# A decoder layer on one core: where the loads between the retention heads stand, gated values in quarters, mixing's weights before the last head

## The chip, the core and the metric

The kernel runs on one core of one Trainium2 chip. The core has five engines with a queue each, and each takes its instructions in the order of its queue: TensorE (PE; its weight loads are shown as PEld) for matmuls, VectorE (DVE), ScalarE (ACT), GpSimd (POOL), and SyncE (SP), which here only issues DMA transfers. ScalarE and GpSimd can issue transfers too; such an issue stands in the engine's own queue and is shown as ACTq or POOLq. The metric is the device time of one execution in microseconds (us), as a median over runs. The trace comes from one more execution under the hardware profiler.

## The reference

One layer of a decoder for 512 prompt tokens and 8 sequences of 8 new tokens, 576 tokens in all, width 1024, float32. Between two gated feed-forward blocks of half weight stands the token mixing, which is the part that matters here:

```python
z = h @ w_in
u, v, q, k, rv, rg, ga, gb = jnp.split(z, SPLIT_POINTS, axis=-1)
u = jax.nn.gelu(u)
v = layer_norm(jax.nn.gelu(v), gm_ln_g, gm_ln_b)
o_a = u * chunk_spatial_mix(v, gm_ws, gm_bs)
qh = rotary(q.reshape(B, L, RET_HEADS, RET_DK), pos)
kh = rotary(k.reshape(B, L, RET_HEADS, RET_DK), pos) * (RET_DK ** -0.5)
o_r, S_new = retention(qh, kh, vh, S0)
o_b = head_rms(o_r).reshape(B, L, RET_V).astype(h.dtype) * jax.nn.silu(rg)
merged = jax.nn.sigmoid(ga) * (o_a @ w_a) + jax.nn.sigmoid(gb) * (o_b @ w_b)
```

Retention has 8 heads with keys of 128 and values of 256 columns and works in chunks of 128 tokens: scores with a decay inside a chunk, and a state of 128 x 256 from chunk to chunk. The new tokens start from a given state for each sequence and head (8 x 8 states of 128 x 256) and give back the new ones. The spatial mixing multiplies the normalised values v in 8 groups of 128 columns by a masked 128 x 128 matrix over the tokens of a chunk, adds a bias, and multiplies by u.

## The kernel before, in words

Products keep float32 accuracy by splitting each operand into a high part, rounded to the matmul's format (fp32r), and the rest. A product is three matmuls: high x high, high x rest, rest x high. A weight is loaded into a raw buffer (`load_raw`, L139, SP's queue; three buffers `wraw`), ScalarE writes its high part (L150) and VectorE its rest (L151) into one of four buffers `whl`. Results are split the same way by `split` (L158 on ScalarE, L159 on VectorE). `proj` (L447) is the product of a weight with 288 token columns at a time; two halves make 576.

The first part of the kernel, up to about 760 us, makes the adaptive gains, the first feed-forward block and the products for q, k, rg, ga and gb, which it writes to DRAM. The last part, from about 1238 us, is the product with w_a, the merge, w_o and the second feed-forward block. The change lies between, in the loop over the heads (L1599) and in the mixing behind it (L1627 to L1694). A turn of the loop for head `hd` does:

- the two weight pieces of the value projection (`load_w`, L1601), and the fetch of the next head's four row tensors q, k and two of rg (`fetch`, L1279, SP's queue);
- the rotary of this head's q and k (`rotary`, L1284 to L1286 on VectorE, L1287 on GpSimd), ahead of the value projection, except for head 0, where it stands behind it;
- the value projection itself (`values_of`, L1309 for four blocks of 128 tokens, L1320 for the new tokens);
- what is left of the head before (`finish(prev)`), and then this head's `core`, a generator in eight pieces. Its pieces are put between the products that run beside it: after each group of matmuls `tick` counts an assumed time down, and a generator whose pause has run out gives its next piece. The pieces: scores (L1337, L1339), decayed q and k, transposes; states of the chunks (L1399, L1404); product with the old states of the new tokens (L1415); outputs for each half of 128 columns (L1428 to L1443, copies L1432, L1448, squares L1449, gate L1488); sum of squares (L1451) and its split; its column sums (L1461), the new states (L1472, L1476) and their way out (L1477, GpSimd's queue), the reciprocal root (L1465); and the scaling of the outputs (L1481 to L1489) with their split into `OB`;
- beside it the products: for heads 0 and 1 the values v (`values`, L1532), for heads 2, 4 and 6 the product of two finished heads with w_b (`out_b`, four pieces), for heads 3 and 5 four pieces of u (`gate_u`); for head 7 nothing.

The states of the next head (`states`: one constant tile, L1292, and four tiles of 256 KB, L1296) are issued at the end of `core` in ScalarE's queue. Their four buffers are those that the old states leave by L1477. `values` loads four pieces of 512 columns x 2 blocks, which fill all four `whl`. `layer_norm` starts behind head 1's values, loads gain and bias for each half (L1569, L1570), normalises ten tiles (L1575, L1578) and writes them to DRAM.

Behind the loop the mixing loads the ten value tiles back (L1632), then a mask, the small and the large mixing weights and the bias (L1634 to L1641). `masks` (L1645, L1647) is called between the two pieces of `out_b` for head 6, and `mix` for eight groups (L1662, L1664 matmuls, L1666, L1670 bias, L1674 product with u on GpSimd, then `split`) runs while head 7's core ends; the two pieces of `out_b` for head 7 come behind groups 5 and 6.

Most row-sized tiles come from one pool of 36 slots (`slot`). The order on the engines' queues isn't simply the source's: a planner takes the traced instructions, gives each an assumed cost and, going through that assumed time, puts the earliest in the source that could start next on each engine; a tile is given to an instruction when one is free in that plan. On the chip each queue then keeps that order, whatever the real times are.

## Time and profile before

| what | us |
|---|---|
| runs: median (lowest, highest), 3 runs | 1743.71 (1738.88, 1744.86) |
| the profiled execution's own time | 1748.43 |
| its span, from the first to the last instruction | 1746.6 |
| TensorE busy in the span | 1670.1 |
| stretch of the heads and the mixing, 759.9 to 1238.0 | 478.1 |
| TensorE busy before it, of 759.9 | 740.7 |
| TensorE busy behind it, of 508.6 | 497.1 |
| mean granted TensorE clock | 0.978 |

How to read the rows: a row of the timeline has the start, the duration of the merged group, engine, line, operation, tiles written and read, shape and count; in brackets the time that the engine sat idle before it and what released it. Rows of stretches have the length, the busy time of the five engines in the order PE, PEld, DVE, ACT, POOL with their counts, the granted clock as a share of full speed, the busy share of the DMA engines and GB/s. Rows of waits have the total, the number and the longest. The durations of merged matmuls overlap by a little at their ends, so the distance between starts is the better measure of their pace.

### The profile page before, as it was taken

Reading aid. Unit: us, or ns where it says so; the run is one execution under the profiler, and the core shown is the slowest. Engines: PE = TensorE matmul, PEld = TensorE weight load, DVE = VectorE, ACT = ScalarE, POOL = GpSimd, SP = SyncE. Lnnn points to the kernel's source line nnn. Section 1 sums busy time; section 2 is a strip of 40 time slices with the busy share of each in tenths; the row PEclk is TensorE's granted clock in tenths of the full one; section 3 lists DMA queues with packets and bytes.
Section 4 is the critical chain, followed back from the end, with each engine's and each line's share of the span. In section 5 each row is a group of like instructions: output and inputs, shape, how many; then the busy total and the mean of one; then the engine's idle time right before and its main releaser. Section 6 shows DMA issues by size and latency. Waiting matters only on the chain.

```text
span 1746.6 us, 30913 instructions
## 1 busy us (share of the span) xinstructions
PE 1670.1 (96%) x12324; PEld 1590.7 (91%) x12324; DVE 1150.3 (66%) x1813; ACT 787.6 (45%) x1335; POOL 304.4 (17%) x384
## 2 busy tenths in 40 slices
PE   7999999999999999989989999977999999999997
PEld 4889999999999998978788899977999999999997
DVE  6857847675787776745577545555566968676773
ACT  5534515344655556533344444433335625334454
POOL 0000000001211010022334344444512000000002
PEclk9999999999999999999999999987999999999999
DMA  9443544434366676673266475695951232222331
GB/s 304 138 133 97 151 127 124 132 86 133 95 200 205 209 208 183 200 237 107 72 224 205 155 162 160 149 236 130 275 174 52 70 100 85 85 85 86 96 97 55
DMA packets 299314, 254.41 MB, mean 146 GB/s; under 512 B 13721, under 2 KB 256665, under 8 KB 299170
## 3 DMA queue, kind: packets, MB, share of 16 engines
q1 hardware_dynamic: 273922, 198.20, 37.9%
q0 software_dynamic: 14320, 43.33, 9.4%
q10 hardware_dynamic: 10928, 10.91, 2.0%
q8 instruction: 96, 1.57, 0.4%
q14 instruction: 48, 0.39, 0.1%
HBM read 207.01 MB, written 45.38 MB: 145 GB/s over the span
## 4 chain that ended last, share of the span: by engine, by line
PE 74%; issue 9%; DMA 7%; DVE 5%; POOL 3%; ACT 2%; SPq 0%; POOLq 0%; ACTq 0%; DVEq 0%
PE ps L613 35%; PE ps L447 28%; PE ps L1309 2%; PE ps L1532 2%; PE ps L269 2%; DMA ada<-in_w_ada_dram 1%; PE ps L1399 1%; DMA ut_ret_state_sample_dram<-S 1%; DMA c<-x1d 1%; DMA xa<-in_w_ada_dram 1%; DMA v<-vd 1%; POOL c L1287 1%; POOL c L1488 1%; DMA S<-in_state_ret_dram 1%; DMA c<-in_gm_ln_g_dram 1%
## 5 line engine op out<-in xcount | busy, mean ns | idle before, releaser
L613 PE MATMUL ps<-xa,whl 128*128 128x288 f32 x3000 | 428.2, 297 | 4.5 <-ACT whl L631 1.4
L613 PEld LDWEIGHTS ps<-xa,whl 128*128 128x128 f32 x3000 | 408.9, 189 | 17.1 <-issue 5.9
L613 PE MATMUL ps<-xs,whl 128*128 128x288 f32 x2040 | 294.9, 297 | 2.1 <-ACT sn L622 1.9
L613 PEld LDWEIGHTS ps<-xs,whl 128*128 128x128 f32 x2040 | 279.0, 189 | 15.0 <-ACT sn L622 7.0
L641 DVE TENSOR_TENSOR whl<-wraw,whl 128x1024 fp32r<-128x1024 f32 x192 | 234.7, 1225 | 54.0 <-ACT whl L631 48.6
L631 ACT CAST whl<-wraw 128x1024 fp32r<-128x1024 f32 x192 | 200.2, 1048 | 104.6 <-DVE wraw L755 61.7
L447 PE MATMUL ps<-c,wd 128*128 128x288 f32 x1824 | 245.7, 295 | 0.0
L447 PEld LDWEIGHTS ps<-c,wd 128*128 128x128 f32 x1824 | 242.8, 188 | 2.7 <-issue 1.7
L447 PE MATMUL ps<-c,whl 128*128 128x288 f32 x1368 | 195.9, 302 | 8.3 <-ACT c L158 8.0
L447 PEld LDWEIGHTS ps<-c,whl 128*128 128x128 f32 x1368 | 189.0, 194 | 10.3 <-ACT c L158 8.4
L434 POOL TENSOR_TENSOR x<-x,s 128x64 f32<-128x64 f32 x72 | 35.4, 492 | 822.1 <-DVE s L433 822.0
L428 DVE SCALAR_TENSOR_TENSOR x<-ps,gate,x 128x288 f32<-128x288 f32 (+1 forms) x128 | 61.1, 481 | 118.3 <-PE ps L447 118.3
L151 DVE TENSOR_TENSOR whl<-wraw,whl 128x1024 fp32r<-128x1024 f32 x56 | 78.5, 1402 | 73.0 <-ACT whl L150 72.5
L622 ACT COPY sn<-ps 128x288 f32<-128x288 f32 x195 | 77.4, 399 | 104.1 <-PE ps L613 103.2
L914 ACT CAST wd<-wraw 128x640 fp32r<-128x640 f32 (+2 forms) x58 | 45.3, 781 | 110.3 <-PE ps L447 106.2
L1309 PE MATMUL ps<-whl,xx 128*128 128x256 f32 x768 | 89.4, 277 | 0.0
L1309 PEld LDWEIGHTS ps<-whl,xx 128*128 128x128 f32 x768 | 88.8, 188 | 0.2
L150 ACT CAST whl<-wraw 128x1024 fp32r<-128x1024 f32 x56 | 58.3, 1049 | 49.1 <-PE ps L1320 16.1
L613 PE MATMUL ps<-xs,whs 128*128 128x288 f32 x480 | 70.4, 295 | 0.0
L631 ACT CAST whs<-wraw 128x512 fp32r<-128x512 f32 x62 | 38.4, 620 | 65.9 <-PE ps L613 59.0
L613 PEld LDWEIGHTS ps<-xs,whs 128*128 128x128 f32 x480 | 65.8, 188 | 0.8 <-issue 0.8
L919 DVE TENSOR_TENSOR wd<-wraw,wd 128x640 fp32r<-128x640 f32 (+2 forms) x58 | 54.0, 931 | 10.8 <-ACT wd L914 10.7
(282 smaller groups left out, 2246.0 us busy)
## 6 DMA issues: line engine op xcount, KB each, us to landing
ada<-in_w_ada_dram SPq DMA_DIRECT2D x56, 512.0 KB, 4.4
wraw<-in_w_in_dram SPq DMA_DIRECT2D x96, 256.0 KB, 4.1
wraw<-in_w_gate_dram SPq DMA_DIRECT2D x88, 256.0 KB, 3.0
wraw<-in_w_up_dram SPq DMA_DIRECT2D x88, 256.0 KB, 3.9
wraw<-in_w_in_dram SPq DMA_DIRECT2D x32, 512.0 KB, 5.1
wraw<-in_w_down_dram SPq DMA_DIRECT2D x32, 384.0 KB, 3.7
accd<-c POOLq DMA_DIRECT2D x40, 288.0 KB, 4.8
wraw<-in_w_down_dram SPq DMA_DIRECT2D x32, 320.0 KB, 3.3
```

Of the source, the lines that this page charges most:

```text
L150: ACT.copy(out=hi, in_=raw)
L151: (eng or DVE).tensor_tensor(out=lo, in0=raw, in1=hi.bitcast(F32), op=ALU.subtract)
L428: DVE.scalar_tensor_tensor(out=x[:, o:o + w], in0=ps[:, :w], scalar=g[:, c, 0:1], in1=x[:, o:o + w], op0=ALU.mult, op1=ALU.add)
L434: return lambda: POOL.tensor_tensor(out=x[:, NP:T], in0=x[:, NP:T], in1=u, op=ALU.add)
L447: PE.matmul(ps[:, :H], lhsT=s[:, k, c0:c0 + P], rhs=m[:, HALF[h]], start=k == 0 and z == 0, stop=k == kc - 1 and z == 2,)
L613: PE.matmul(ps[:, :H], lhsT=s[:, j * P:(j + 1) * P], rhs=m[:, j, :], start=fresh and j == 0 and z == 0, stop=j == 3 and z == 2, skip_group ...
L622: ACT.copy(out=t, in_=ps[:, :H])
L631: ACT.copy(out=hl[:, 0], in_=src)
L641: DVE.tensor_tensor(out=hl[:, 1], in0=src, in1=hl[:, 0].bitcast(F32), op=ALU.subtract)
L914: ACT.copy(out=hl[:, 0], in_=self.raw[c])
L919: DVE.tensor_tensor(out=lo, in0=self.raw[c], in1=hi.bitcast(F32), op=ALU.subtract)
L1309: PE.matmul(ps[:, :DV], lhsT=s, rhs=m, start=i == 0, stop=i == 23)
```

## The change

States are issued on SP's queue for every head, behind the two weight loads of the value projection. The fetch of the next head's rows stands behind the first of the products beside the core, and the rotary of the next head behind the second last of four products (behind both, for heads 0 and 1). `finish(prev)` stands at the end of the turn. The layer norm starts with head 2's products. `values` computes a tile in two parts of 256 columns, each with two weight pieces of 4 blocks x 256 columns; a value tile's slot is taken with its first part, and its statistics come with the second. The mask, mixing weights and biases are loaded at the end of head 6's turn, both `masks` stand ahead of `out_b` for head 6, and every second product with u goes to VectorE. What is computed is the same.

```diff
-    def states(hd, queue):
+    def states(hd):
...
-        queue.dma_start(out=hc, in_=a["hconst"][hd])
+        nc.sync.dma_start(out=hc, in_=a["hconst"][hd])
...
-            queue.dma_start(out=t, in_=a["state_ret"][0, 2 * j:2 * j + 2, hd].rearrange("b d e -> d b e"))
+            nc.sync.dma_start(out=t, in_=a["state_ret"][0, 2 * j:2 * j + 2, hd].rearrange("b d e -> d b e"))
...
             split(OB[e][0], OB[e][1], o[e])
-        if hd + 1 < HEADS:
-            states(hd + 1, nc.scalar)
         yield 0.0
...
-    def values(i):
-        ws = [load_w(win, 2 * kk, 2, V0 + i * 512, 512) for kk in range(4)]
+    def values(i, z):
+
+        ws = [load_w(win, 4 * kk, 4, V0 + i * 512 + z * 256, 256) for kk in range(2)]
+        cl = slice(z * 256, (z + 1) * 256)
...
-                w = ws[kx // 2]
+                w = ws[kx // 4]
...
                     PE.matmul(
-                        ps, lhsT=s, rhs=m[:, kx % 2, :], start=kx == 0 and z == 0,
-                        stop=kx == KC - 1 and z == len(terms) - 1,
+                        ps[:, :256], lhsT=s, rhs=m[:, kx % 4, :], start=kx == 0 and y == 0,
+                        stop=kx == KC - 1 and y == len(terms) - 1,
                     )
             m = P if n < 4 else NS
-            t = slot([m, 512])
+            if z == 0:
+                v[n, i] = slot([m, 512])
+            t = v[n, i][:, cl]
             if n < 4:
-                ACT.activation(out=t, in_=ps, func=AF.Gelu_apprx_tanh)
+                ACT.activation(out=t, in_=ps[:, :256], func=AF.Gelu_apprx_tanh)
             else:
-                ACT.copy(out=t, in_=ps[NS:P])
-                DVE.tensor_tensor(out=t, in0=ps[0:NS], in1=t, op=ALU.add)
+                ACT.copy(out=t, in_=ps[NS:P, :256])
+                DVE.tensor_tensor(out=t, in0=ps[0:NS, :256], in1=t, op=ALU.add)
                 ACT.activation(out=t, in_=t, func=AF.Gelu_apprx_tanh)
-            v[n, i] = t
-            DVE.bn_stats(out=tks["stats"][0:m, n, i, :], in_=t)
-            tick(24 * 0.216)
+            if z:
+                DVE.bn_stats(out=tks["stats"][0:m, n, i, :], in_=v[n, i])
+            tick((24 if n < 4 else 16) * 0.109)
...
-    states(0, nc.sync)
-    coming, prev, OBs = fetch(0), None, []
+    states(0)
+    rows, prev, OBs = {0: fetch(0)}, None, []
+
+    def beside(hd):
+
+        if hd < 2:
+            yield lambda: values(hd, 0)
+            yield lambda: values(hd, 1)
+        elif hd % 2 == 0:
+            for j in range(4):
+                yield lambda j=j: out_b((hd - 2, hd - 1), j)
+        elif hd < HEADS - 1:
+            for g in range(2 * hd - 6, 2 * hd - 2):
+                yield lambda g=g: gate_u(g)
+
     for hd in range(HEADS):
-        mine = coming
         wv = [load_w(win, 4 * i, 4, RV0 + hd * DV, DV) for i in range(2)]
-        coming = hd + 1 < HEADS and fetch(hd + 1)
         if hd:
-            for x in mine[:2]:
-                rotary(x)
+            states(hd)
         rv, rvs = values_of(hd, wv)
         if hd == 0:
-            for x in mine[:2]:
+            for x in rows[0][:2]:
                 rotary(x)
-        else:
+        OBs.append([])
+        q, k, *gates = rows.pop(hd)
+        prev = core(hd, q, k, gates, rv, rvs, OBs[hd])
+        start(prev, 0.5)
+        if hd == 2:
+            start(layer_norm(), 1.0)
+        work = list(beside(hd))
+        for i, f in enumerate(work):
+            f()
+            if i == 0 and hd + 1 < HEADS:
+                rows[hd + 1] = fetch(hd + 1)
+            if i == len(work) - 2 and i:
+                for x in rows[hd + 1][:2]:
+                    rotary(x)
+        if len(work) == 2:
+            for x in rows[hd + 1][:2]:
+                rotary(x)
+        if hd + 1 < HEADS:
             finish(prev)
-        OBs.append([])
-        prev = core(hd, mine[0], mine[1], mine[2:], rv, rvs, OBs[hd])
-        start(prev, 0.5)
-        if hd < 2:
-            values(hd)
-            if hd:
-                start(layer_norm(), 1.0)
-        elif hd % 2 == 0:
-            for j in range(4):
-                out_b((hd - 2, hd - 1), j)
-        elif hd < 6:
-            for g in range(2 * hd - 6, 2 * hd - 2):
-                gate_u(g)
+        if hd == HEADS - 2:
+            gmc = slot([P, P + NS])
+            nc.sync.dma_start(out=gmc, in_=a["gmc"])
...
+            for i in range(2):
+                nc.sync.dma_start(out=wm[i], in_=a["gm_wsT"][:, 4 * i:4 * i + 4])
+                nc.sync.dma_start(out=bs[i], in_=a["gm_bs"][0, 4 * i:4 * i + 4].partition_broadcast(P))
...
-    gmc = slot([P, P + NS])
-    nc.sync.dma_start(out=gmc, in_=a["gmc"])
...
+    masks(0)
+    masks(1)
...
-        POOL.tensor_tensor(out=t, in0=t, in1=us[g], op=ALU.mult)
+        (POOL if g % 2 else DVE).tensor_tensor(out=t, in0=t, in1=us[g], op=ALU.mult)
...
     out_b((HEADS - 2,), 0)
-    masks(0)
     out_b((HEADS - 2,), 1)
-    masks(1)
```

13 lines of the change are left out of this document (5 added, 8 removed).

## The prediction

> **What bounds the kernel now.** I read the page first, then the busy time of stretches of one head each, then what TensorE waited for, then the rows around each long wait.
>
> ```profile
> span 1746.6 us, 30913 instructions
> PE 1670.1 (96%) x12324; PEld 1590.7 (91%) x12324; DVE 1150.3 (66%) x1813; ACT 787.6 (45%) x1335; POOL 304.4 (17%) x384
> ```
>
> TensorE is busy 96% of the span, so only its waits can be won, and the lower clock behind them. Each stretch below starts with a head's value projection (L1309); the last one holds head 7 and the mixing.
>
> ```profile
> core 0: us, PE busy (x) PEld busy (x) DVE busy (x) ACT busy (x) POOL busy (x), PEclk, DMA share, GB/s
> 759.90:817.50 57.60, 53.46 (x332) 45.38 (x331) 24.29 (x35) 18.53 (x32) 19.09 (x26) 0.94 0.38 125
> 817.50:872.30 54.80, 51.37 (x329) 43.85 (x328) 32.97 (x47) 21.43 (x36) 16.25 (x16) 1.00 0.38 123
> 872.30:937.00 64.70, 54.66 (x409) 52.54 (x408) 52.75 (x84) 25.05 (x46) 25.95 (x35) 0.89 0.68 221
> 937.00:986.30 49.30, 49.30 (x411) 48.08 (x410) 25.96 (x34) 21.62 (x38) 17.55 (x18) 1.00 0.49 159
> 986.30:1041.20 54.90, 51.03 (x411) 49.49 (x410) 30.00 (x40) 23.76 (x44) 24.09 (x24) 0.97 0.64 157
> 1041.20:1090.50 49.30, 49.30 (x411) 48.08 (x410) 27.89 (x36) 21.54 (x38) 19.29 (x19) 1.00 0.57 174
> 1090.50:1143.70 53.20, 51.06 (x410) 49.46 (x410) 30.06 (x40) 23.86 (x44) 23.42 (x24) 0.97 0.66 161
> 1143.70:1238.00 94.30, 72.17 (x512) 67.83 (x511) 47.22 (x76) 34.90 (x72) 44.73 (x40) 0.86 0.79 182
> ```
>
> Heads 3 and 5 show a head without a wait: 49.30 us, TensorE busy throughout, granted clock 1.00. Heads 2, 4 and 6 put as many products beside the core (409 to 411 records in all five), so what they take above 49.30 is waiting and clock: 15.4, 5.6 and 3.9 us.
>
> ```profile
> PE ps L1337 <- POOL c L1287: 12.9, 6, 5.7
> PE ps L1399 <- DVE c L1339: 10.0, 1, 10.0
> PE ps L447 <- ACT c L158: 8.0, 2, 7.3
> ```
>
> These are TensorE's longest waits there: on rotated rows (L1287), on a score multiply (L1339), on splits by ScalarE (L158).
>
> **States on SP's queue, rotary inside the products.** Head 4 shows the chain that both edits cut:
>
> ```profile
> 984.27 7.85 DMA ut_ret_state_sample_dram<-S
> ...
> 990.85 0.37 ACTq L1296 DMA_DIRECT2D S<-in_state_ret_dram  x1
> 991.25 1.28 ACT L1591 ACT_TABLE_LOAD   x1 [6.83 <-issue]
> ...
> 996.33 0.75 DVE L1284 TENSOR_TENSOR c<-c,rope 64x576 f32<-64x576 f32 x1
> ...
> 1004.67 1.21 PE L1337 MATMUL ps<-c,c 128*128 128x128 f32 x8 [3.87 <-POOL c L1287]
> ```
>
> The loads of the next states (L1296) stand in ScalarE's queue until the old states, on their way out from 984.27 to 992.12, free the first buffer. ScalarE stands 6.83 us, its splits are late, VectorE gets to the rotary at 996.33, GpSimd ends it late, and TensorE waits 3.87 us for it. Afterwards the five loads per head (35 for heads 1 to 7, at 0.37 us of issue each) wait on SP, and the rotary (per row tensor three VectorE instructions, one on GpSimd) stands behind the third of four products: one product, a value projection (12.8 us by the rows of head 3 below) and the first piece of the next product lie between it and its use. VectorE has room for it there (30.00 us busy of 54.90). Behind the waiting state load on SP stand later weight loads and the next row fetch, and behind those the splits. I cost that wait at nothing, since the weights run ahead:
>
> ```profile
> 953.61 28.04 SPq L139 DMA_DIRECT2D wraw<-in_w_b_dram  x4
> ...
> S<-in_state_ret_dram ACTq DMA_DIRECT2D x28, 256.0 KB, 4.3
> ...
> wraw<-in_w_b_dram SPq DMA_DIRECT2D x16, 512.0 KB, 4.7
> ```
>
> All four loads of head 4's product had been issued by 981.65, before the old states began to leave at 984.27. What it costs without that cover is rival 3. The row fetch, now behind the first product, has two products until the rotary: 96 matmuls at 0.132 us (3.16/24, rows of head 3 below), 12.6 us. So heads 4 and 6 lose their 5.6 and 3.9: **-9.5 us**.
>
> **Layer norm starts with head 2's products.** Head 2's 15.4 us are a rotary wait as above, 5.68 us by the longest of L1287's waits, and this:
>
> ```profile
> 919.95 1.41 DVE L1575 SCALAR_TENSOR_TENSOR c<-c,mv,c 128x512 f32<-128x512 f32 x2 [5.97 <-DMA c<-in_gm_ln_g_dram]
> ...
> 925.45 0.75 DVE L1451 TENSOR_TENSOR c<-c,c 128x576 f32<-128x576 f32 x1
> ...
> 926.95 0.46 PE L1461 MATMUL ps<-c,onesr 128*128 128x288 f32 x1 [3.53 <-ACT c L158]
> ```
>
> VectorE waits 5.97 us for the second half's gains, and the core's L1451 stands behind them. By its pauses (40 us in all) the layer norm now ends beside head 3, whose VectorE is the least busy (25.96 of 49.30). But its first half falls on the core's second half, ten value slots stay held longer, and head 2's VectorE is the fullest (52.75). Between all of the 15.4 gone and only the rotary's part gone (5.68 and about 3 for the clock, an estimate from the 5.4 that the head lost beyond its waits of about 10), I keep 5 us: **-10.4 us**.
>
> **Values in quarters.** Weights come in pieces that use two of four split buffers instead of all four, so the next piece can be split early. Now:
>
> ```profile
> 781.16 2.08 PE L1532 MATMUL ps<-whl,xx 128*128 128x512 f32 x4 [3.56 <-DVE whl L151]
> 783.44 2.08 PE L1337 MATMUL ps<-c,c 128*128 128x128 f32 x8 [0.20 <-POOL c L1287]
> ...
> 796.28 5.86 PE L1532 MATMUL ps<-whl,xx 128*128 128x512 f32 x24
> 802.08 0.43 PE L1428 MATMUL ps<-scs,rvs 64*128 64x64 f32 x2
> ...
> 937.01 11.04 PE L1309 MATMUL ps<-whl,xx 128*128 128x256 f32 x96
> 947.90 2.06 PE L1320 MATMUL ps<-whl,hs 128*128 128x256 f32 x16
> 949.79 3.32 PE L447 MATMUL ps<-xx,whl 128*128 128x288 f32 x24
> 952.95 1.05 PE L1337 MATMUL ps<-c,c 128*128 128x128 f32 x8
> ...
> 958.11 1.89 PE L1399 MATMUL ps<-c,c 128*128 128x256 f32 x8
> ```
>
> The matmuls, by starts: 512 columns take 5.80/24 = 242 ns; the same kind with 256 takes 10.89/96 = 113 ns, or 1.89/16 = 118 ns on the sample rows. Per head 96 + 16 wide ones (27.1 us, the 16 taken at the same rate) become 192 + 32 narrow ones (21.8 + 3.8 = 25.6): -1.5 us. Per head five more GELUs, a copy on ScalarE and an add on VectorE come with the pieces, beside ScalarE 18.53 and VectorE 24.29 us busy of 57.60. A head with values and no wait is then 49.3, less eight gate products' halves (8 x 3.16 = 25.3 us), plus 25.6: 49.6 us. Head 1 goes from 54.8 to 49.6, head 0 from 57.6 at best to 49.6. Head 0 has no earlier product, though: its rotary still follows its value projection, L1337 was free at 783.44 only, and a narrow row of products gives it 24 x 0.113 = 2.7 us of cover instead of 5.8. I leave half of its 8.0: **-9.2 us** for both.
>
> By the Trainium skill ("TensorE: Matmul & The Clock Gate", Back-to-back issue gap) a warm matmul takes N/2.4 + 2.5 ns, a figure for isolated ones, so splitting one of 512 columns costs 2.5 ns more (218 against 216). By that the quarters would cost about 0.3 us per head and not win 1.5, and the sum would be 3.6 us higher; the rows above are 242 and 2 x 113, and I go by them.
>
> **Mixing's loads sooner, masks first.**
>
> ```profile
> 1152.71 6.21 SPq L1632 DMA_DIRECT2D v<-vd  x10
> ...
> 1173.23 0.69 DVE L1645 TENSOR_TENSOR c<-c,c 128x512 f32<-128x512 f32 x1 [11.91 <-DMA c<-in_gm_wsT_dram]
> ...
> 1174.77 3.75 PE L1399 MATMUL ps<-c,c 128*128 128x256 f32 x8 [9.96 <-DVE c L1339]
> 1177.96 5.13 PE L447 MATMUL ps<-c,whl 128*128 128x288 f32 x30
> ```
>
> The mask weights queue behind the ten value loads, VectorE waits 11.91 us with a mask in hand, and the score multiply behind it holds TensorE 9.96 us. The clock adds 3.75 - 1.89 (head 3's row above) and 5.13 - 30 x 0.138 (3.32/24): 2.8 us. The 13 loads now stand on SP before head 7's weights, at 0.62 us of issue each (6.21/10) about 8 us of a queue that the weights run ahead of by more; seven of 36 slots are held a head longer, which I cost at nothing between 0 and one wait of 3.5. The ten mask instructions fall where the rotary was. **-12.8 us**.
>
> **Every second gating product on VectorE.**
>
> ```profile
> L1674 POOL TENSOR_TENSOR c<-c,c 128x576 f32<-128x576 f32 x8 | 14.4, 1794 | 11.3 <-DVE c L1670 7.1 <-issue 4.2
> ```
>
> Four of eight leave GpSimd (1.79 us each) for VectorE (0.75, as the same shape at L1451), in the chain that ends in the 7.3 us wait on L158. Two of them lie before that wait's end: from -2 x 1.04 to +1.5, I take **-1 us**.
>
> **Sum.** -9.5 - 10.4 - 9.2 - 12.8 - 1 = -42.9; against it I set one new wait of about 3 us (an estimate, from the 3.53 of head 2): -39.9. The profiled execution took 1748.43 us; its sum is 1708.5. The median of the runs is 1743.71, 4.7 lower, so **1704 us**.
>
> **The rivals.**
>
> 1. Everything goes: head 2 reaches 49.3, head 0 49.6, no new wait. 5 + 4 + 3 + 1 more: 1691 us. For it: heads 3 and 5 stand at 49.30. Against: head 0's rotary.
>
> 2. The wait moves into VectorE's queue. Rows come from a fetch issued only two products ahead, and a layer norm or rotary piece that waits for its transfer holds the core's pieces, as 5.97 did in head 2. Three such waits at 15.4 - 5.68 - 3 = 6.7 each give 20 back: 1724 us. For it: VectorE works in order, as L1575 and L1645 show. Against: 12 us against landings of 4 to 5.
>
> 3. The slower side: SP is held by the states, and the first weights of each product come after them. From 992.12: state landing 4.3, weights 4.7, splits 1.05 and 1.23 to 2.3: 1003.4 to 1004.5, where TensorE wants them at 999.1, so 4.3 to 5.4 us, and about 1.9 for the clock as at L1399, at seven boundaries. It outweighs 42.9 us from 4.2 us of wait on; at 5.4 it is +51 - 42.9: 1752 us. For it: the source puts the states ahead of the product's weights. Against: the loads issued by 981.65. The Trainium skill ("DMA: Bandwidth & Descriptors", Anatomy of one DMA) says that the wait is always the issuing sequencer's, never the DMA engine's; ScalarE's 6.83 us agree, and SP would stand as long.
>
> 4. The change doesn't do what it says: the planner sorts each engine's instructions by its own costs (L1645 ran before L1339, which the source has first), and rotary stays late. Then only heads 0 and 1, mixing and GpSimd's part remain, 23 us: 1721 us.
>
> **How the numbers follow.** Forecast 0.48 (1696 to 1713), rival 1 0.15, rival 2 0.20, rival 4 0.08, rival 3 0.09. The range, 1688 to 1732, holds all but rival 3 and some of the tails. A measurement of this kernel tells about 0.3%, 5.2 us, from no change: faster (under 1738.5) 0.86, same 0.06, slower 0.08.
>
> **What would show it.** Right: no ScalarE row with an idle "issue" before a table load at a head's start; L1337 without a wait in heads 1 to 7; stretches of heads 1, 4 and 6 near 49.5; L1399 of head 7 without a wait; 256-column rows of L1532 near 113 ns. Wrong: a wait of L1309 or of a product's first matmul on L151 after late state loads (rival 3), or of L1461 behind VectorE waiting for rows or gains (rival 2). If the stretch from 759.9 to 1238.0 (478 us) is not at least 30 us shorter, the prediction is wrong.

## The result, and the profile after

The changed kernel took 1726.1 us (median of four runs, 1723.93 to 1729.52) against 1742.1 for the kernel before on the same chip (1738.88 to 1744.86): a ratio of 0.9911, 95% interval 0.9885 to 0.9936. The forecast was 1704 us. It is 0.9% faster than the kernel before and 22 us slower than forecast: the change gave 16 us where 39.9 were counted.

The first lines of the page of the changed kernel; TensorE's busy time fell by 13.4 us, its share of the span stayed:

```profile
span 1722.2 us, 31384 instructions
PE 1656.7 (96%) x12548; PEld 1590.4 (92%) x12548; DVE 1153.4 (67%) x1819; ACT 792.9 (46%) x1347; POOL 301.2 (17%) x380
```

Busy time by stretches of one head each, as in the prediction (stretch and its length; then TensorE, weight loads, VectorE, ScalarE, GpSimd; then granted clock, DMA share, GB/s):

```profile
757.40:807.28 49.88, 49.88 (x443) 48.75 (x442) 28.07 (x40) 22.19 (x39) 19.81 (x26) 1.00 0.50 167
807.28:857.06 49.78, 49.78 (x442) 48.65 (x441) 32.66 (x48) 22.87 (x42) 17.35 (x15) 1.00 0.43 137
857.06:914.38 57.32, 52.18 (x411) 50.18 (x409) 46.72 (x71) 22.89 (x45) 25.19 (x28) 0.94 0.55 177
914.38:970.09 55.71, 50.76 (x410) 49.31 (x409) 32.51 (x44) 23.25 (x39) 21.91 (x24) 0.97 0.51 172
970.09:1020.40 50.31, 49.56 (x411) 48.11 (x409) 31.93 (x43) 22.81 (x43) 25.00 (x25) 1.00 0.74 187
1020.40:1069.68 49.28, 49.28 (x411) 48.06 (x410) 25.17 (x34) 23.14 (x39) 16.72 (x18) 1.00 0.52 157
1069.68:1119.98 50.30, 49.55 (x410) 48.10 (x409) 32.59 (x43) 22.71 (x43) 24.48 (x25) 1.00 0.73 183
1119.98:1213.28 93.30, 69.97 (x513) 66.49 (x511) 45.45 (x79) 35.79 (x72) 35.20 (x37) 0.87 0.80 190
```

Heads 0 and 1 run without a wait, heads 4 and 6 nearly so. Head 2 is shorter, but head 3, one of the two that had no wait before, now takes 55.71 us. Head 7 with the mixing takes 93.30 us where it took 94.3: the largest term of the sum brought 1 us. The eight stretches together fell from 478.1 to 455.9 us.

The longest of TensorE's waits in them (us in total, times, longest): the wait on rotated rows (L1337) has gone from the list, and other waits head it.

```profile
PE ps L447 <- ACT c L158: 9.6, 2, 8.8
PE ps L1461 <- ACT c L158: 9.0, 2, 6.3
PE ps L447 <- DVE rvs L1325: 7.2, 1, 7.2
PE ps L1375 <- POOL h L1370: 5.0, 1, 5.0
PE ps L447 <- DVE S L1476: 2.5, 3, 1.0
```

The timeline around head 7's start (1119.98), SP's queue (SPq), GpSimd, VectorE and TensorE, explains the third row. L139 at 1079.53 loads head 7's value weights, L1477 writes the old states out, L1296 loads the new ones, L1643 to L1650 are the mixing's loads, L1662 the masks, L1658 the values:

```profile
1079.53 4.89 SPq L139 DMA_DIRECT2D wraw<-in_w_in_dram  x2
...
1119.06 2.97 POOL L1477 DMA_DIRECT2D ut_ret_state_sample_dram<-S  x4
...
1122.07 3.68 SPq L1296 DMA_DIRECT2D S<-in_state_ret_dram  x4
...
1125.85 0.42 SPq L139 DMA_DIRECT2D wraw<-in_w_a_dram  x1
1126.32 0.57 SPq L1643 DMA_DIRECT2D c<-in_gmc_dram  x1
1126.94 8.31 SPq L1647 DMA_DIRECT2D c<-in_gm_wsT_dram  x8
...
1135.36 0.37 SPq L1649 DMA_DIRECT2D c<-in_gm_wsT_dram  x1
...
1137.26 9.13 SPq L1658 DMA_DIRECT2D v<-vd  x10
1138.07 0.69 DVE L1662 TENSOR_TENSOR c<-c,c 128x512 f32<-128x512 f32 x1 [11.73 <-DMA c<-in_gm_wsT_dram]
...
1143.96 0.42 DVE L1325 TENSOR_TENSOR rvs<-ps,h 128x256 f32<-128x256 f32 x1
...
1144.44 5.14 PE L447 MATMUL ps<-c,whl 128*128 128x288 f32 x24 [7.15 <-DVE rvs L1325]
```

The mixing's loads do not go ahead of head 7: its value weights had left SP 42 us before them, and the first of them leaves 6.3 us after the head's start, behind the states and a weight load. The states themselves wait for the old ones to leave. Eight small loads come next, and the first large mask weight (L1649) leaves 15.4 us after the start. In the kernel before, whose head 7 starts at 1143.70, the first load had left 5.9 us and the first large mask weight (L1640) 21.4 us after the start:

```profile
1149.59 0.46 SPq L1634 DMA_DIRECT2D c<-in_gmc_dram  x1
...
1165.10 0.49 SPq L1640 DMA_DIRECT2D c<-in_gm_wsT_dram  x1
```

So the large weights do leave 6.0 us sooner. But VectorE comes to the masks sooner still: it begins to wait for them 6.4 us after the head's start (1138.07 less 11.73), where it had begun 17.6 us after it (1173.23 less 11.91, in the prediction's rows). It stands 11.73 us, as long as before, and L1325, which had stood in front of the masks, now stands behind them. The wait changed its victim, from L1339 (9.96 us) to L1325 (7.15 us), and TensorE's waits on ScalarE's splits (L158) in this stretch grew from 11.5 to 15.9 us in total.

The same in heads 2 and 3, with the layer norm's gains (L1571 their load, L1577 their first use):

```profile
884.28 1.04 SPq L1571 DMA_DIRECT2D c<-in_gm_ln_g_dram  x1
...
892.50 1.41 DVE L1577 SCALAR_TENSOR_TENSOR c<-c,mv,c 128x512 f32<-128x512 f32 x2 [8.74 <-DMA c<-in_gm_ln_g_dram]
...
920.71 0.46 SPq L1571 DMA_DIRECT2D c<-in_gm_ln_g_dram  x1
...
927.42 1.41 DVE L1577 SCALAR_TENSOR_TENSOR c<-c,mv,c 128x512 f32<-128x512 f32 x2 [6.69 <-DMA c<-in_gm_ln_g_dram]
...
937.17 0.69 PE L1375 MATMUL ps<-ident,h 128*128 128x128 f32 x2 [4.95 <-POOL h L1370]
```

Each half is loaded just before its use, and the use begins 6.7 to 8.2 us after the issue. The second one falls into head 3, whose L1375 waits 4.95 us for a copy on GpSimd (L1370) that came late beside it.

### The profile page after: what moved, and what is told of

It is laid out like the page before. It is cut to its first block, busy times and chain, and to the rows that moved or that the text cites. A ratio compares the mean times of both kernels' runs of the same rounds, so it can differ in the third digit from the quotient of the medians.

```text
span 1722.2 us, 31384 instructions
## 1 busy us (share of the span) xinstructions
PE 1656.7 (96%) x12548; PEld 1590.4 (92%) x12548; DVE 1153.4 (67%) x1819; ACT 792.9 (46%) x1347; POOL 301.2 (17%) x380
## 4 chain that ended last, share of the span: by engine, by line
PE 79%; issue 8%; DMA 6%; DVE 4%; POOL 2%; ACT 1%; SPq 1%; POOLq 0%; DVEq 0%; ACTq 0%
PE ps L613 36%; PE ps L447 28%; PE ps L1309 4%; PE ps L1532 3%; PE ps L269 2%; DMA ada<-in_w_ada_dram 1%; DMA wraw<-in_w_a_dram 1%; PE ps L1320 1%; DMA xa<-in_w_ada_dram 1%; PE ps L1399 1%; PE ps L1437 1%; DMA c<-x1d 1%; DVE whl L641 0%; ACT whl L631 0%; DMA c<-in_gm_ln_g_dram 0%
## 5 line engine op out<-in xcount | busy, mean ns | idle before, releaser
L151 DVE TENSOR_TENSOR whl<-wraw,whl 128x1024 fp32r<-128x1024 f32 x56 | 78.0, 1393 | 71.5 <-ACT whl L150 71.1
L150 ACT CAST whl<-wraw 128x1024 fp32r<-128x1024 f32 x56 | 58.7, 1048 | 27.9 <-PE ps L447 16.1
L919 DVE TENSOR_TENSOR wd<-wraw,wd 128x640 fp32r<-128x640 f32 (+2 forms) x58 | 54.1, 932 | 10.6 <-ACT wd L914 10.4
```

What stands on the lines that cost most here:

```text
L150: ACT.copy(out=hi, in_=raw)
L151: (eng or DVE).tensor_tensor(out=lo, in0=raw, in1=hi.bitcast(F32), op=ALU.subtract)
L919: DVE.tensor_tensor(out=lo, in0=self.raw[c], in1=hi.bitcast(F32), op=ALU.subtract)
```

## The experiments

Theory: transfers that land late hold VectorE's order, in head 3 by gains, in head 7 by masks, and take back what the edits win. Rivals: the mixing is bound by the serial chain of head 7's core; VectorE's load bounds heads 2 and 3; the parts did win, and the loss is elsewhere. The kernel before had medians of 1742.6, 1742.6, 1741.7 and 1742.9 us in the four comparisons. "7+" below is the stretch of head 7 and the mixing.

**The mixing as before.**

```diff
-        if hd == HEADS - 2:
-            gmc = slot([P, P + NS])
-            nc.sync.dma_start(out=gmc, in_=a["gmc"])
...
             nc.sync.dma_start(out=v[n, i], in_=vd[0:m, i, n])
+    gmc = slot([P, P + NS])
+    nc.sync.dma_start(out=gmc, in_=a["gmc"])
...
-    masks(0)
-    masks(1)
...
     out_b((HEADS - 2,), 0)
+    masks(0)
     out_b((HEADS - 2,), 1)
+    masks(1)
```

> The changed kernel with the mixing's loads and masks put back to where they stood before (loads behind the ten value loads, masks around the two pieces of the last output product); everything else as changed. Theory (the masks first in VectorE's order, and the value and w_a loads that the 13 loads push back, give back what was to be won): head 7 and the mixing take 92 to 96 us against 93.3 in the changed kernel and 94.4 before, with one long wait on L1339 near 10 us again; time 1723 to 1730 us, so this part of the change is worth nothing. Rival (the part did win its 12.8 us and the loss lies elsewhere): the stretch is 105 us or more, time 1738 us.

1725.95 us, ratio 0.9909 (0.9882 to 0.9935); 7+ took 91.40 us, a little less than expected, with 9.3 us again on L1339. This part of the change is worth nothing.

**The mixing's tiles in a place of their own.** All but one of them get a pool beside the slots, and the loads move in the source from the end of head 6's turn to the end of head 5's.

```diff
-NSLOT = 36
+NSLOT = 32
+        mxp = pool(tok_pools, "mx")
+        tks["mx"] = lambda shape: mxp.tile(shape, F32, name=nm("mx"))
...
-        if hd == HEADS - 2:
-            gmc = slot([P, P + NS])
+        if hd == 5:
+            mxt = tks["mx"]
+            gmc = mxt([P, P + NS])
...
-            wm, bs = ([slot([P, 4, P]) for _ in range(2)] for _ in range(2))
-            ws8, wd8 = slot([NS, 8, LS]), slot([NS, 8, NS])
+            wm, bs = ([mxt([P, 4, P]) for _ in range(2)] for _ in range(2))
+            ws8, wd8 = mxt([NS, 8, LS]), slot([NS, 8, NS])
```

> The changed kernel, but the mixing's tiles have a place of their own (the pool of slots shrinks from 36 to 32), so that their 13 loads wait for no slot and can go at the start of the stage, and the masks long before head 7. Theory: the 7.2 us wait on L1325 behind the masks goes, the clock loss of 1.8 us behind it too, and with the loads out of the queue the w_a weights come in time, which takes 3 of the 6.35 us on L1461: head 7 and mixing take 80 to 84 us against 93.3, time 1714 to 1717 us. Rival (the stretch is bound by the serial chain of head 7's core and the products by L1694, with too few matmuls to cover it): the wait moves on to the two waits on L158 (8.9 and 6.4 us), the stretch stays over 89 us, time 1722 to 1726 us. The smaller pool could cost some waits in heads 0 to 6; these stretches would show it.

1707.54 us, 0.9796 (0.9773 to 0.982). The stretch 7+ and its two waits:

```profile
1118.39:1196.33 77.94, 68.32 (x514) 64.95 (x512) 45.05 (x77) 34.84 (x72) 34.96 (x37) 0.91 0.83 204
```

```profile
PE ps L447 <- ACT c L158: 6.3, 2, 5.6
PE ps L1463 <- ACT c L158: 3.0, 1, 3.0
```

15.4 us less than in the changed kernel, more than the 12.8 of the prediction. Without a slot to wait for, the planner itself moved the loads and the large masks into head 0 (771 to 789 us). The move in the source isn't what did it: in the kernel before (below) the same tiles, with the loads left where they stood, bring them into head 0 as well. The serial chain remains (both waits on L158), but it was not the bound: the waits there became smaller, not larger.

**The control: 32 slots alone.**

```diff
-NSLOT = 36
+NSLOT = 32
```

> The changed kernel with a pool of 32 slots and nothing else: the control for the own tiles. If the own tiles' gain comes from the loads and the masks, this is no faster than the changed kernel: head 7 and mixing 92 to 96 us, time 1724 to 1732 us. Rival (another pool size gives the planner another order, and that order was the gain): head 7 and mixing under 85 us, time under 1715 us.

1729.17 us, 0.9919 (0.9898 to 0.9939), 7+ 97.16 us, a little over the expected range: the gain is not the pool's size. (Head 3 fell to 51.9 us here as in the run above, so that part of the shift in heads 2 and 3 does come from the pool.)

**Own tiles in the kernel before.** The same tiles in the kernel before, with the loads at their old place in the source.

```diff
-NSLOT = 36
+NSLOT = 32
...
             nc.sync.dma_start(out=v[n, i], in_=vd[0:m, i, n])
-    gmc = slot([P, P + NS])
+    mxt = tks["mx"]
+    gmc = mxt([P, P + NS])
...
```

> The kernel before with one edit: the mixing's tiles in a place of their own (pool of 32 slots), their loads at the start of the stage. If the predicted 12.8 us were there to be won and only the way did not reach them, the wait of 10 us on L1339 goes and head 7 and mixing fall from 94.4 to 77 to 83 us; time 1725 to 1731 us against 1742. Rival (they can be won only beside the other edits): over 88 us, time 1736 us or more.

1733.31 us, 0.9939 (0.9922 to 0.9956). The loads left in head 0 here too (778 to 789 us), the wait on the score multiply (L1339 in the kernel before) is gone, and 7+ fell from 94.3 us by 15.4:

```profile
1148.33:1227.26 78.93, 68.43 (x513) 64.75 (x512) 46.90 (x74) 34.08 (x72) 43.15 (x40) 0.91 0.80 195
```

The time fell by 9.6 us only, less than expected. Part of the difference is the first profile of before: against the second one, below, 7+ fell by 12.2 us. The 12.8 us were in the mixing to be won, and the change's way did not reach them.

**The gains early.**

```diff
-            lng, lnb = slot([P, 512]), slot([P, 512])
+            lng, lnb = tks["ln"][i]
             cl = slice(i * 512, (i + 1) * 512)
-            nc.sync.dma_start(out=lng, in_=a["gm_ln_g"][0, cl].partition_broadcast(P))
-            nc.sync.dma_start(out=lnb, in_=a["gm_ln_b"][0, cl].partition_broadcast(P))
...
+        if hd == 1:
+            tks["ln"] = []
+            for i in range(2):
+                lng, lnb = slot([P, 512]), slot([P, 512])
...
+                tks["ln"].append((lng, lnb))
```

> The changed kernel, but the four loads of the layer norm's gains and biases go at the end of head 1 into slots of their own instead of at the start of each half in heads 2 and 3. Theory (the halves wait in VectorE's order for gains that take 7 to 9 us to land): VectorE's waits of 8.74 and 6.69 us on the gains go, head 3 falls from 55.7 to 49.5 to 51 us and head 2 from 57.3 to 52 to 55 us; time 1714 to 1720 us. Rival (VectorE's load is the bound: the layer norm's 20 operations of 0.7 us stand in front of the core's): heads 2 and 3 together lose less than 3 us, time 1723 to 1726 us.

1716.13 us, 0.9843 (0.9817 to 0.9869). Heads 2 and 3:

```profile
859.83:914.41 54.58, 50.63 (x410) 48.82 (x409) 53.28 (x82) 23.00 (x45) 31.26 (x35) 0.98 0.71 222
914.41:964.44 50.03, 50.03 (x410) 48.81 (x409) 24.40 (x32) 23.10 (x39) 15.30 (x17) 0.98 0.47 151
```

That is 8.4 us less than 57.32 + 55.71, with VectorE busier in head 2 than before (53.28 against 46.72): the wait for the transfer cost the time, not VectorE's load.

**The layer norm started where it was.**

```diff
-        if hd == 2:
-            start(layer_norm(), 1.0)
         work = list(beside(hd))
...
+        if hd == 1:
+            start(layer_norm(), 1.0)
         if hd + 1 < HEADS:
             finish(prev)
```

> The changed kernel with the layer norm started behind head 1's values, as before, and not with head 2's products. Theory (the place of the start only chooses which head waits for the gains): head 3 goes back to 49.3 us and head 2 up to 61 to 64 us, together 110 to 113 against 113.0; time 1723 to 1727 us. Rival (the later start did win in head 2 what was predicted, and head 3's loss has another cause): together 118 us or more, time 1731 us or more.

1724.43 us, 0.9907 (0.9886 to 0.9928). Heads 2 and 3 took 62.87 and 49.28 us, 112.2 together against 113.0, and the time is the same within its noise: the later start only moved the wait from one head to the next.

**The states on ScalarE again.**

```diff
             split(OB[e][0], OB[e][1], o[e])
+        if hd + 1 < HEADS:
+            states(hd + 1, nc.scalar)
...
-        if hd:
-            states(hd)
```

> The changed kernel with the states put back on ScalarE's queue at the end of each core; the rotary stays inside the products. Theory as predicted (the state loads hold ScalarE up, then the splits, then TensorE): ScalarE's stall of 6 to 7 us before the table load comes back at heads 3, 5 and 7 starts, heads 4 and 6 take 52 to 55 us against 50.3, time 1732 to 1738 us. Rival (only the place of the rotary mattered, and the stall is covered by products whose splits are done): heads 4 and 6 stay at 49.3 to 50.5 us; head 3 and the mixing can gain, since SP is free of the states: the gains and the 13 loads go 4 us sooner; time 1718 to 1726 us.

1724.73 us, 0.9912 (0.9889 to 0.9935); heads 4 and 6 at 50.29 us each. Around head 7's start (1121.11) of this kernel, ScalarE, VectorE and SP:

```profile
1123.37 1.05 ACT L150 CAST whl<-wraw 128x1024 fp32r<-128x1024 f32 x1 [5.85 <-DMA ut_ret_state_sample_dram<-S]
...
1124.92 1.22 DVE L151 TENSOR_TENSOR whl<-wraw,whl 128x1024 fp32r<-128x1024 f32 x1
...
1126.17 0.37 SPq L139 DMA_DIRECT2D wraw<-in_w_a_dram  x1
1126.59 0.70 SPq L1643 DMA_DIRECT2D c<-in_gmc_dram  x1
```

ScalarE stands for the old states again, 5.85 us, and no cost shows in the time: the rotary is done by then. And SP, free of the states, is no sooner at the mixing's loads (5.5 us after the head's start against 6.3): ahead of them stands a weight load that waits for a buffer freed by VectorE's L151 (it goes 0.03 us after L151 ends), and L151 stands in VectorE's order behind the end of the core. In the changed kernel L151 ends at 1125.00 and the states' issue at 1125.75, so there the states are the last to hold the queue; without them L151 holds it nearly as long.

**The rotary at the start of the head again.**

```diff
         if hd:
             states(hd)
+            for x in rows[hd][:2]:
+                rotary(x)
...
-            if i == len(work) - 2 and i:
-                for x in rows[hd + 1][:2]:
-                    rotary(x)
...
```

> The changed kernel with the rotary of heads 1 to 7 put back to the start of each head, ahead of its value projection; the states stay on SP. Theory (VectorE and GpSimd end it in 6 to 7 us, the value projection lasts 13 us, and without ScalarE's stall nothing makes it late): heads 4 and 6 reach 49.3 to 50 us, even without the waits of 0.75 us on L1476 that the early rotary brought, heads 1 and 2 within 2 us: time 1721 to 1727 us. Rival (the place of the rotary is what removed the waits on L1287): those waits return at 3 to 5 us in heads 2, 4 and 6, time 1733 to 1740 us.

1716.96 us, 0.9851 (0.9823 to 0.9879): undoing this edit makes the kernel about 9 us faster. Heads 3, 4 and 7+:

```profile
917.78:968.97 51.19, 49.50 (x410) 48.05 (x409) 34.00 (x44) 23.17 (x39) 23.07 (x24) 1.00 0.52 181
968.97:1018.25 49.28, 49.28 (x410) 48.07 (x409) 29.90 (x40) 22.91 (x43) 22.33 (x24) 1.00 0.71 177
1116.81:1204.77 87.96, 70.58 (x513) 66.93 (x512) 49.67 (x80) 35.45 (x72) 37.73 (x36) 0.88 0.83 197
```

The rows before head 7 show why. In the changed kernel the rotary stands in VectorE's order in front of the core's last steps (L1476):

```profile
1117.55 2.47 DVE L1476 SCALAR_TENSOR_TENSOR S<-S,ps 128x512 f32<-128x512 f32 x4
...
1118.28 1.87 PE L447 MATMUL ps<-c,whl 128*128 128x288 f32 x12 [0.75 <-DVE S L1476]
```

With the rotary late, in the kernel of this run:

```profile
1111.69 2.47 DVE L1476 SCALAR_TENSOR_TENSOR S<-S,ps 128x512 f32<-128x512 f32 x4
...
1118.10 1.23 DVE L151 TENSOR_TENSOR whl<-wraw,whl 128x1024 fp32r<-128x1024 f32 x1
...
1120.27 0.41 SPq L139 DMA_DIRECT2D wraw<-in_w_a_dram  x1
1120.73 1.00 SPq L1639 DMA_DIRECT2D c<-in_gmc_dram  x1
...
1132.25 0.69 DVE L1658 TENSOR_TENSOR c<-c,c 128x512 f32<-128x512 f32 x1 [7.68 <-DMA c<-in_gm_wsT_dram]
```

L1476 comes 5.1 us before head 7 instead of 2.4, so TensorE never waits for its banks; the old states leave sooner, L151 and all of SP's queue move forward too, and the mixing's loads leave 3.9 us after the head's start instead of 6.3. In head 3 the load of the gains leaves sooner too (3.0 against 6.3 us after the start), and VectorE does rotary work in the meantime. The masks (L1658) still hold VectorE, for 7.68 us and in front of the last rotary instruction, so that TensorE waits 4.6 us for rotated rows in head 7 in place of the 7.15 us on L1325.

**The states' queue alone, in the kernel before.**

```diff
-        if hd + 1 < HEADS:
-            states(hd + 1, nc.scalar)
...
         coming = hd + 1 < HEADS and fetch(hd + 1)
         if hd:
+            states(hd, nc.sync)
```

> The kernel before with one edit: the states are loaded on SP's queue at the start of each head, behind its weights and the next rows, and not on ScalarE's at the end of the core. Rotary, values, layer norm, mixing as before. Theory from the last runs (either edit alone, the queue or the place of the rotary, takes away the wait on rotated rows): heads 4 and 6 fall from 54.9 and 53.2 to 49.3 us, head 2 by 3 to 6 us, no wait on L1287 over 1 us in these heads; time 1726 to 1733 us against 1742.6. Rival (the rotary before the value projection is late by its own operations, and the early place is needed too): heads 4 and 6 stay over 52 us, time 1737 us or more.

1735.44 us, 0.9957 (0.9942 to 0.9972). Heads 4 and 6 are without a wait:

```profile
983.14:1032.43 49.29, 49.29 (x411) 48.07 (x410) 29.91 (x40) 22.88 (x43) 22.31 (x24) 1.00 0.73 176
1081.70:1130.99 49.29, 49.29 (x411) 48.08 (x410) 29.92 (x40) 22.88 (x43) 21.64 (x24) 1.00 0.72 176
```

So in heads 4 and 6 the wait on rotated rows needs both causes, ScalarE's stall and the late place, and either edit alone removes it. In head 2 a wait of 6.6 us on L1287 stayed: there the rotary stands behind the last of head 1's values on VectorE. That head fell by 1.9 us only, and the time missed its range.

**The values in halves again.** The function of before, with 512 columns, rows fetched ahead of it and the rotary behind it.

```diff
-    def values(i, z):
-        ws = [load_w(win, 4 * kk, 4, V0 + i * 512 + z * 256, 256) for kk in range(2)]
+    def values(i):
+        ws = [load_w(win, 2 * kk, 2, V0 + i * 512, 512) for kk in range(4)]
...
-            yield lambda: values(hd, 0)
-            yield lambda: values(hd, 1)
+            yield lambda: values(hd)
...
+        if hd < 2:
+            rows[hd + 1] = fetch(hd + 1)
         for i, f in enumerate(work):
```

> The changed kernel, but the gated values are computed in halves of 512 columns as before (four weight pieces that take all four split buffers), the row fetch ahead of them and the rotary behind them. Theory (the quarters bring 1.5 us a head by faster columns and the rest by splits that can run ahead): heads 0 and 1 go back from 49.9 and 49.8 to 56 to 58 and 53 to 55 us, time 1735 to 1739 us. Rival (the stalls of heads 0 and 1 went with the states' queue and the place of the rotary, the quarters give the columns alone): 51 to 52 us each, time 1728 to 1730 us.

1735.83 us, 0.996 (0.9942 to 0.9977): 1735.8 against 1726.1 us, so the quarters, with the places of fetch and rotary that go with them, are worth about 9 us by the times, as forecast (9.2). Head by head it looks otherwise: 51.28, 53.76, 60.45 and 53.94 us for heads 0 to 3, only 5.4 us more than in the changed kernel in heads 0 and 1, of the 12.7 that these had lost (this profiled execution took 1729.06 us, below the median). In head 1 TensorE is busy 51.18 us against 49.78 (1.4 us of the columns' 1.5) and waits 2.0 us for splits; in head 2 a wait of 4.9 us on L1287 comes back.

**The gating products all on GpSimd.**

```diff
-        (POOL if g % 2 else DVE).tensor_tensor(out=t, in0=t, in1=us[g], op=ALU.mult)
+        POOL.tensor_tensor(out=t, in0=t, in1=us[g], op=ALU.mult)
```

> The changed kernel with all eight gating products on GpSimd again. Predicted: 1 us between -1.5 and +2.1 for this edit, so 1725 to 1728 us; head 7 and mixing 93 to 96 us. Rival (the products on VectorE stand ahead of the chain that ends head 7's core, and cost more there than GpSimd saves): under 1722 us.

1727.04 us, 0.9908 (0.9891 to 0.9925): no difference that can be told from the changed kernel in the time. The stretch 7+, 90.43 us, came out under its range, and why is not known.

**Combinations.** Own tiles and early gains together (the two diffs above):

> The changed kernel with both of the last finds together: the mixing's tiles in a place of their own with loads at the start of the stage (36 slots become 32), and the layer norm's gains loaded at the end of head 1. If the two waits are separate causes, heads 2 and 3 take 104 to 106 us together as with the early gains alone, head 7 and mixing 77 to 79 us as with the own tiles alone: stage 432 to 435 us, time 1703 to 1707 us. Rival: the two add, as 10 us from the gains and 18.5 us from the mixing's tiles by their times: 1697 to 1699 us. If the smaller pool of slots makes the early gains wait, it is slower than the own tiles alone: over 1708 us.

1706.46 us, 0.9799 (0.9774 to 0.9824), the eight stretches 433.5 us. They do not add: own tiles alone had already shortened heads 2 and 3. With the rotary put back as well (the diff above):

> The mixing's tiles in a place of their own and the gains early, as together before, and the rotary back at the start of each head. If the early rotary is what costs 1 us in heads 4 and 6 and the waits on L1476, heads 4 to 6 take 49.3 us each, head 2 54 to 57, head 3 49.3, head 7 and mixing 74 to 78: stage 428 to 432 us against 433.5, time 1699 to 1703 us. Rival (its gain of 9 us came from heads 3 and 7 being moved against their loads, which the other two edits have already taken): 1704 to 1707 us.

1697.89 us, 0.9748 (0.9732 to 0.9765), a little under its range, the fastest of all and faster than both kernels. In the stretches head 2 came out under its range and 7+ a little over it. Its head 2 and 7+, and the sum of the eight stretches:

```profile
860.55:913.31 52.76, 49.88 (x411) 48.14 (x410) 47.43 (x79) 22.49 (x45) 26.03 (x34) 1.00 0.74 235
...
1110.42:1189.04 78.62, 68.63 (x514) 65.11 (x512) 50.50 (x78) 34.81 (x72) 35.78 (x36) 0.91 0.81 199
sum 428.15, PE 415.28 PEld 402.91 DVE 272.75 ACT 194.11 POOL 177.48; mean PE 51.91 PEld 50.36 DVE 34.09 ACT 24.26 POOL 22.18
```

Heads 3 to 6 take 49.27 to 49.29 us each. Last, on top of that, the layer norm beside head 3 with its gains loaded at the end of head 2, and the first product with w_a ahead of head 7's output product (the loads of the sums, `gate_b`, follow it):

```diff
-        if hd == 2:
+        if hd == 3:
             start(layer_norm(), 1.0)
-        if g in (5, 6):
-            out_b((HEADS - 1,), g - 5)
...
+        if pr == [0]:
+            for j in range(2):
+                out_b((HEADS - 1,), j)
+            gate_b(0)
+            gate_b(1)
```

> As the run before, and two steps further: the gains load at the end of head 2 and the layer norm starts with head 3's products, whose VectorE was the least busy (25.96 of 49.30 us before); and the first product with w_a goes ahead of head 7's output product, which waits 6 us for the end of the core, with the loads of the sums behind it. If VectorE's load is what is left of head 2, head 2 falls from 55 to 57 to 49.3 to 51 us and head 3 stays under 51; head 7 and mixing up to the long run lose 3 to 4 us more: time 1688 to 1694 us. Rival (head 3's core is late instead, and ten values held for longer leave too few slots): heads 2 and 3 together over 104 us, time 1697 to 1702 us.

1700.95 us, 0.9775 (0.9755 to 0.9795): not faster. Heads 2 and 3 took 52.44 and 49.99 us. In head 2 VectorE is now busy 34.61 us and the head is hardly shorter than with 47.43, so VectorE's load is not what is left there. What is left are waits of TensorE on the splits before the column sums, 1.8 us on L158 and 0.9 on L159; why these are late stays open. The wait for head 7's core became waits of the later products on their weight splits (L150, L151, 0.7 to 1.3 us each).

**A second profile of the kernel before.**

> The kernel before once more, for a second profile. If the stretch of the eight heads is a property of the kernel, it is 477 to 479 us again, and the 5 to 6 us by which the first profiled execution lay above the median came from the stages around it. If the stretch itself varies, it is 470 to 474 us.

The whole stretch in one row:

```profile
761.25:1234.89 473.64, 432.65 (x3210) 404.91 (x3209) 271.54 (x386) 190.98 (x348) 191.62 (x199) 0.95 0.59 167
```

473.6 us against 478.1: head 2 took 60.34 instead of 64.7, 7+ 91.10 instead of 94.3, head 0 60.34 instead of 57.6. One profiled execution is good to a few us in a stretch that has waits. Head 5, which has none, took 49.26 to 49.28 us by its starts in fifteen of the seventeen profiles, and 49.72 in the two with own tiles and the early rotary. That a stretch has no wait need not repeat, though: head 3 of the kernel before took 49.30 us in the first profile and 50.32 in the second, with a wait of 0.8 us on L1287.

## Why the prediction was wrong

By its own terms, profile against profile. It asked for at least 30 us from 478; the stretch lost 22.2. In the last column the times of the single runs are compared, whose intervals are about 4 us to either side; 0 means nothing beyond that.

| term | forecast | stretches, before to after | worth when undone alone |
|---|---|---|---|
| states on SP, rotary in the products | -9.5 | heads 4, 6: -7.5 | states 0; rotary +9 (it costs) |
| layer norm with head 2 | -10.4 | head 2: -7.4, head 3: +6.4 | 0 |
| values in quarters | -9.2 | heads 0, 1: -12.7 | about -9 |
| mixing's loads, masks first | -12.8 | 7+: -1.0 with the next term | 0 |
| products on VectorE | -1 | in the row above | 0 |
| a new wait | +3 | head 3 and L1325, counted above | |

**Mixing, the largest miss (12.8 us with the next term).** The step that failed is "the 13 loads now stand on SP before head 7's weights", with "seven of 36 slots are held a head longer, which I cost at nothing". I read their place in the source as their place in time. On SP they stand behind head 7's value weights, its states and another weight load, and the first of them left no sooner after the head's start than in the kernel before (6.3 us against 5.9). Their number was priced too low as well: from the first issue to the last they take 10.8 us and not 8, and the eight small ones stand in front of the large mask weights that VectorE waits for. The large ones gained 6.0 us all the same, but the masks moved up by 11.3 us in VectorE's order, so VectorE waited as long as before and L1325 took the place of L1339. "The ten mask instructions fall where the rotary was" counted their work and not what stands behind them. Against the second profile of before (91.1 us) this stretch did not win at all.

The price was about right: with tiles of their own the stretch lost 15.4 us here and 12.2 to 15.4 in the kernel before. So it was the tiles' slots that kept the planner from placing the loads sooner; what held the queue in front of them was the states, which wait for the old ones to leave behind L1476, and next to them a weight load that waits for L151, behind the core's end on VectorE.

**Layer norm.** "The layer norm now ends beside head 3, whose VectorE is the least busy" counted instructions and not their transfer. The second half's gains wait 6.69 us there as they had waited 5.97 in head 2. With the loads early, heads 2 and 3 lose 8.4 us more, 9.4 in all against the 10.4 that were forecast.

**States and rotary.** The chain was read rightly (in heads 4 and 6 both edits cut it), and the mark that L1337 is without a wait in heads 1 to 7 came true. The forecast gave both edits one sum and did not ask whether one is enough. One is, in these two heads, and the other has a price: "VectorE has room for it there" is true of its busy time, 31.93 of 50.31 us, but not of its order. The rotary stands in front of L1476 (TensorE waits 0.75 us) and of L151, and SP's queue moves back 2.4 us before head 7. The Trainium skill ("DMA: Bandwidth & Descriptors", Anatomy of one DMA) puts such a wait on the issuing sequencer. The traces agree: with the states on its queue ScalarE stood 5.85 us, and in the changed kernel SP stands up to 4.5 us for them.

**Quarters.** The sum was right by the times, about 9 us, but luck has a part in it. Of the 12.7 us that heads 0 and 1 lost, 5.4 came back with the halves; the rest came with the other edits, to which the prediction gave nothing there, and the record does not say with which. The half kept for head 0's rotary was too careful: head 0 took 49.88 us, 0.3 above the 49.6 worked out. The columns themselves were read rightly: TensorE's busy time in head 1 is 49.78 us with quarters and 51.18 with halves. By the Trainium skill's figure for isolated matmuls ("TensorE: Matmul & The Clock Gate", Back-to-back issue gap: 2.5 ns more per split matmul) the quarters would have been a small loss. The measurement decides against it for this shape.

**Products on VectorE.** Within the bounds given, below what can be measured.

**The rivals.** Rival 2 is what happened, nearly at its time (1724): waits in VectorE's order of 8.74, 6.69 and 11.73 us, though for gains and masks, never for rows. That its three equal prices of 6.7 us add up so near to the result is partly luck, since other terms of the sum missed too. It had 0.20; its mechanism stood quoted in the prediction, in L1575's 5.97 us and L1645's 11.91 us, and the change moved each use along with its load, or further. Its mark came true in head 2, where L1461 waits 2.7 us for a split behind the gains. The mark for head 7, L1399 without a wait, came true as well and proved nothing, since L1325 had the wait. Rival 3 did not come: TensorE waits for no weight split (L151) in these stretches. Rival 4 came in part: the rotary ran where the source has it, but the planner put head 7's weights and states ahead of the mixing's loads, which the source has first. Of the baseline, the profiled execution of before lay 4.5 us above a second one in this stretch, so some of the 22.2 us is not the change's: the medians differ by 16.

## What to carry to other kernels

A load moved up in the source has moved in time only if its tile, its queue and the instruction ahead of it in that queue let it; look for the release that it waits for, and give it a place of its own before anything else. Where two edits cut the same chain, price each one alone: the second may win nothing more, and can cost. And before an operation is put where an engine "has room", list what stands behind it in that engine's order, down to the buffers which those instructions free.

## What the runs showed of the hardware

- The time that a load holds SP did not go by its bytes: issuing one of the eight loads of 8 x 8 x 8 values takes 0.67 us (median in three kernels, 0.67 to 0.83), one of the ten value loads, which carry up to 128 times as much, 0.40 us in the kernel before. The 8.31 us of the eight in the changed kernel hold a wait of 2.5 us besides.
- A gain row spread over 128 partitions (128x512) is used 6.7 to 8.2 us after its issue, where the state and weight loads of 256 and 512 KB in the prediction's rows take 4.3 and 4.7. The spreading is not shown to be the cause: the large mask weights, of 256 KB and not spread, took 8.0 us in the kernel before.
- Head 5, a stretch without waits, took 49.26 to 49.28 us in fifteen of seventeen profiles of different kernels, while stretches with waits differed by up to 4.4 us (head 2) between two executions of the same program.
